# Masked products of a chunk: two heads on the array's row halves, a bank for each head

## The chip, the core and the metric

The kernel runs on one core of one Trainium2 chip. A core has a matrix engine (TensorE, PE in the profile, with its weight loads shown apart as PEld), a vector engine (VectorE, DVE), an activation engine (ScalarE, ACT), a general engine (GpSimd, POOL) and a queue that issues most of the DMAs (SyncE, SP). TensorE writes to PSUM, a small memory of 128 partitions in banks of 512 float32 columns; VectorE and ScalarE read it from there. The metric is device microseconds of one execution, as a median of several.

## What is computed

One inference step of a two-layer hybrid decoder: a convolution layer, then a layer of RWKV-7 time mixing, each followed by a squared-ReLU MLP. The prompt has 1024 tokens and 16 meta tokens in front, and 8 decoded sequences add one token each. The change lies in the time mixing of the prompt, the recurrence over tokens with 16 heads of size 64:

```python
def _wkv7_step(S, inp):
    r_t, w_t, k_t, v_t, kk_t, a_t = inp
    sa = jnp.einsum('bhvk,bhk->bhv', S, -kk_t)
    S = (S * w_t[:, :, None, :] + sa[..., None] * (kk_t * a_t)[:, :, None, :]
         + v_t[..., None] * k_t[:, :, None, :])
    y = jnp.einsum('bhvk,bhk->bhv', S, r_t)
    return S, y
```

The kernel doesn't step through the tokens. It takes them in 17 chunks (the 16 meta tokens, then 16 chunks of 64), and within a chunk it works with 64 x 64 matrices of products between tokens, masked to be triangular.

## The kernel before

**Layout.** The model's 1024 features are 8 blocks of 128 partitions (KT = 8). A block holds two heads: head q = 0 on partitions 0 to 63, head q = 1 on 64 to 127 (HALF[0] and HALF[1]). What a mixer stage computes for a chunk is written to the DRAM tensors d_ab (four 64-column vectors for each block), d_v and d_n, and read back by the recurrence.

**Stages.** The work before about 1100 us is the convolution layer and its MLP. Then the mixer runs over four token groups (`mixer_in`, whose projections are L865), and between its matmuls a `tick` advances the recurrence by a few steps. After the mixer the first group of the output projection and the second MLP runs (matmuls at L187 to L189), and its filler advances what is left of the recurrence, the decode step and the normalisation of the outputs. From about 2090 us on only the MLP is left. In these stages the order of TensorE's instructions is the order of the program (a manual schedule for that engine); the other engines' instructions are ordered by the scheduler that builds the kernel.

**One chunk.** `front(c)` loads a chunk and forms its products; `chunk(c)` goes on from there. Each is a generator that yields the credit its last step is worth, and `step(c + 1)` in the chunk before runs pieces of the next chunk's front early. In order:

- `front`: two tiles are loaded, `bk` (L1176 to L1179; stationary, its second head with its column halves swapped) and `xa` (one of two tiles taken in turn, with dimensions partition, block, head, 128 columns). Head q's data goes to `xa[HALF[q], :, q, :]` by SP's DMA (L1175). The other partition half of the same columns has to be zero, because a matmul over 128 partitions would otherwise add the other head's terms: the right 64 columns are zeroed once (L1139), the left 64 for each chunk by two POOL memsets (L1174), since the products below overwrite them.
- The products A (L1192): for each pair of blocks one bank, two matmuls of 128 x 128 weights with 256 moving columns (two heads of 128 columns). Then for each head ACT copies a 32 x 32 corner for both blocks to `no` (L1198) and VectorE writes the masked left half to the other head's partitions in `xa` (L1199); then VectorE writes the masked right halves of both heads to `nr` (L1200). After two of the four pairs the front yields.
- `chunk`: `gg` multiplies `no` with the transposed inverses (L1230; 32 x 32 tiles), `bT` transposes `bk` (L1253), `W` multiplies `xa`'s left half with the state and values `sv` (L1260), `po` (L1230) and `U` (L1276; 64 x 64 tiles) apply the inverse, `S` (L1285) makes the state's increment, and `Y` (L1292 with `xa`'s right half, L1295 with `nr`) the outputs.

**Banks.** A, gg, bT, W, po, U, S and Y, and the transposes of the output's normalisation, share one pool of three PSUM banks (tag "w"). A bank is taken again when all readers of its last tile are done. The mixer's own matmuls have four banks of their own.

**Other users of the queues.** On the mixer's side POOL issues the writes of d_ab, d_n and d_bv (L991, L1030, L1037); in the MLP it forms the low parts of the split weights (L162). `inverses` (L1153, L1154) works on VectorE over d_n and writes d_p.

Of the kernel before, what the change touches and what calls it, by code (L numbers as in the profile page):

```python
# [16 lines left out]
P = 128  # L17
D = 1024
KT = D // P
# [8 lines left out]
HS = 64  # L28
# [17 lines left out]
HALF = [slice(0, HS), slice(HS, P)]  # L46


def hybrid_step(tc, x_prompt, x_sample, state_conv, state_shift, state_wkv, meta_tokens,
# [8 lines left out]
    nc = tc.nc  # L58
    ctx = ExitStack()
    with ctx:  # L60
# [130 lines left out]
        def bank(name, tag="mm"):  # L191
            return cur[tag].tile([P, 512], F32, name=name, tag=tag)
# [191 lines left out]
        with ExitStack() as l0:  # L384
# [261 lines left out]
            with ExitStack() as s:  # L646
# [35 lines left out]
                for i, parts in enumerate((((1, rwkv_w1[0]), (4, rwkv_a1[0])), ((5, rwkv_g1[0]),))):  # L682
                    own, prev = (xin.tile([P, D], F32, name=f"lr{i}{s_}", tag="xt").rearrange("p (k c) -> p k c", k=KT) for s_ in "op")
                    w = P // len(parts)
# [22 lines left out]
        m_ar = masks.tile([P, 2 * HS], F32, name="m_ar")  # L707
# [459 lines left out]
        Q = [slice(32 * i, 32 * i + 32) for i in range(4)]  # L1167
        chunks = {}

        def front(c):  # L1170

            xa = xas[c % 2]
            for q in range(2):
                nc.gpsimd.memset(xa[HALF[1 - q], :, q, :HS], 0.0)  # L1174
                nc.sync.dma_start(xa[HALF[q], :, q, :], d_ab[c, HALF[q], :, 0, :])  # L1175
            bk = w_([P, KT, P], "bk", c)  # L1176
            nc.sync.dma_start(bk[HALF[0]], d_ab[c, HALF[0], :, 1, :])
            for i in range(2):
                nc.sync.dma_start(bk[HALF[1], :, i * HS:(i + 1) * HS], d_ab[c, HALF[1], :, 1, (1 - i) * HS:(2 - i) * HS])  # L1179
            nr, no = w_([P, KT, 2, HS], "nr", c, bufs=2), w_([P, KT, 32], "no", c)  # L1180
            p32 = w_([P, KT, 32], "p32", c, bufs=2)
            nc.sync.dma_start(p32, d_p[c].rearrange("k r t -> r k t"))

            vt = w_([P, KT, HS], "vt", c)
            for q in range(2):
                nc.sync.dma_start(vt[HALF[1 - q]], d_v[c * HS:(c + 1) * HS, :].rearrange("t (k q v) -> q t k v", q=2, v=HS)[q])
            yield RW[0]
            mk = m_ar.unsqueeze(1).broadcast_to([P, 2, P])
            for j in range(0, KT, 2):
                ps = bank(f"A{c}{j}", "w")  # L1190
                for i in range(2):
                    nc.tensor.matmul(ps[:, i * 2 * P:(i + 1) * 2 * P], bk[:, j + i, :],  # L1192
                                     xa[:, j + i].rearrange("p q x -> p (q x)"), start=True, stop=True)
                pv = ps.rearrange("p (i q x) -> p i q x", i=2, q=2)
                for q in range(2):

                    r_k = HALF[1 - q]
                    nc.scalar.copy(no[Q[2 * q], j:j + 2, :], pv[Q[2 * q], :, q, 32:64])  # L1198
                    nc.vector.tensor_mul(xa[r_k, j:j + 2, q, :HS], pv[r_k, :, q, :HS], mk[r_k, :, :HS])  # L1199
                nc.vector.tensor_mul(nr[:, j:j + 2].rearrange("p i q x -> p (i q) x"),  # L1200
                                     ps.rearrange("p (i x) -> p i x", x=P)[:, :, HS:],
                                     m_ar[:, HS:].unsqueeze(1).broadcast_to([P, 4, HS]))
                if j == 2:
                    yield RW[1]
            x32 = w_([P, KT, 32], "x32", c)
            nc.vector.transpose(flat(x32), flat(p32))
            chunks[c] = xa, bk, nr, no, p32, x32, vt
            yield RW[2]

        def step(c):  # L1210

            if c < NCH and c <= st["inv"]:
                if c not in fronts:
                    fronts[c] = front(c)
                next(fronts[c], None)
        fronts = {}

        def chunk(c):

            while c > st["inv"]:  # L1220
                yield None
            yield from fronts.setdefault(c, front(c))
            xa, bk, nr, no, p32, x32, vt = chunks.pop(c)
            sv, uv = st["sv"], st["uv"]
# [420 lines left out]
```

## Time and profile before

| what | us |
|---|---|
| median of 3 runs | 2832.22 |
| lowest and highest | 2829.05, 2835.45 |
| the profiled execution | 2823.53 |
| its span, first to last instruction | 2821.8 |

The mean granted TensorE clock was 0.977 of full speed. The profile's views are read as follows. Each group of instructions has its line in the kernel, its engine, its output and inputs, and its shape. A busy time is the sum over instructions; a wait is the time that an engine stood idle before an instruction, put down to what was done last of all that it waited for. A matmul's record reaches from its start to a modelled end, and neighbouring records overlap, so for the time that a matmul takes of TensorE the distance between starts is used. A float32 matmul leaves two records of matmul and two of weight load.

### The profile page before, as it was taken

The numbers are of one execution on the slowest core, as the hardware profiler recorded it, in microseconds if no ns is written. First come the engines' busy times: TensorE is split into PE (matmuls) and PEld (weight loads), VectorE is DVE, ScalarE is ACT, GpSimd is POOL, SyncE is SP. The second block draws the span as 40 slices with busy tenths as digits, with TensorE's granted clock in tenths as the row PEclk, the third lists the DMA queues.
The fourth block names the chain that finished last, engine by engine and source line by source line (L and its number), as shares of the span: only waits on it lengthen the run. The fifth ranks groups of instructions, "written<-read, shape, count | busy, mean of one in ns | idle before, by whom it ended". The sixth has DMA issues, their size and how long they took to land.

```text
span 2821.8 us, 51604 instructions
## 1 busy us (share of the span) xinstructions
PE 2669.5 (95%) x19594; PEld 2521.3 (89%) x19594; DVE 1785.4 (63%) x3586; ACT 1189.5 (42%) x2235; POOL 1520.2 (54%) x2100
## 2 busy tenths in 40 slices
PE   8999999999999899998999999978899999999998
PEld 8999999999999898786877778777899999999998
DVE  5999999996455545234756455588985564444444
ACT  5545444544354343233454454454444452222223
POOL 6686877887788775022212112375568773333332
PEclk9999999999999999999999999989899999999999
DMA  6663544454445642677767766766665542222211
GB/s 179 179 184 87 156 137 134 137 175 137 140 132 162 191 130 82 198 215 201 185 176 211 186 172 178 203 184 167 170 202 155 170 125 87 68 69 73 70 53 42
DMA packets 615862, 416.42 MB, mean 148 GB/s; under 512 B 104936, under 2 KB 558760, under 8 KB 615614
## 3 DMA queue, kind: packets, MB, share of 16 engines
q1 hardware_dynamic: 565996, 367.36, 46.0%
q10 hardware_dynamic: 41090, 19.93, 2.7%
q0 software_dynamic: 8528, 25.83, 2.6%
q8 instruction: 155, 2.54, 0.4%
q14 instruction: 93, 0.76, 0.1%
HBM read 345.60 MB, written 68.37 MB: 147 GB/s over the span
## 4 chain that ended last, share of the span: by engine, by line
PE 71%; DVE 13%; DMA 6%; issue 4%; ACT 3%; POOL 2%; SPq 0%; ACTq 0%; DVEq 0%; POOLq 0%
PE ps_in L187 8%; PE ps_in L189 8%; PE ps_in L188 8%; PE out L187 8%; PE out L189 8%; PE out L188 8%; PE pk L865 3%; PE pr L865 2%; PE pv L865 2%; POOL wo_lo L162 1%; DVE ni L1154 1%; DVE cv L519 1%; PE ps_o L189 1%; DVE tt L1153 1%; PE ps_o L188 1%
## 5 line engine op out<-in xcount | busy, mean ns | idle before, releaser
L162 POOL TENSOR_TENSOR wo_lo<-wo_raw,wo_hi 128x256 fp32r<-128x256 f32 x736 | 566.5, 802 | 267.5 <-ACT wo_hi L157 253.2
L162 POOL TENSOR_TENSOR wi_lo<-wi_raw,wi_hi 128x256 fp32r<-128x256 f32 x640 | 488.9, 796 | 285.8 <-ACT wi_hi L157 265.4
L187 PE MATMUL out<-hh,wo_hi 128*128 128x352 f32 (+2 forms) x1536 | 503.4, 328 | 19.8 <-DVE h L355 9.3
L355 DVE TENSOR_TENSOR h<-h,out 128x352 f32<-128x352 f32 (+2 forms) x768 | 387.7, 511 | 195.9 <-PE out L189 195.2
L189 PE MATMUL out<-hl,wo_hi 128*128 128x352 f32 (+2 forms) x1536 | 494.0, 324 | 7.2 <-DVE hl L141 7.2
L187 PE MATMUL ps_in<-m_h,wi_hi 128*128 128x352 f32 (+2 forms) x1536 | 496.2, 323 | 1.2 <-DVE h L355 1.2
L188 PE MATMUL out<-hh,wo_lo 128*128 128x352 f32 (+2 forms) x1536 | 495.3, 323 | 0.0
L189 PE MATMUL ps_in<-m_l,wi_hi 128*128 128x352 f32 (+2 forms) x1536 | 494.5, 322 | 0.1
L188 PE MATMUL ps_in<-m_h,wi_lo 128*128 128x352 f32 (+2 forms) x1536 | 492.6, 321 | 0.0
L519 DVE SCALAR_TENSOR_TENSOR cv<-u,wdw,cv 128x352 f32<-128x352 f32 (+2 forms) x720 | 377.2, 574 | 0.7
L157 ACT CAST wi_hi<-wi_raw 128x1024 fp32r<-128x1024 f32 x160 | 167.9, 1050 | 388.6 <-PE out L189 198.3
L157 ACT CAST wo_hi<-wo_raw 128x1024 fp32r<-128x1024 f32 x184 | 192.6, 1049 | 318.4 <-PE out L189 153.6
L187 PEld LDWEIGHTS out<-hh,wo_hi 128*128 128x128 f32 x1536 | 293.0, 191 | 26.0 <-DVE h L355 11.6
L189 PEld LDWEIGHTS out<-hl,wo_hi 128*128 128x128 f32 x1536 | 291.2, 190 | 8.9 <-DVE hl L141 8.8
L188 PEld LDWEIGHTS out<-hh,wo_lo 128*128 128x128 f32 x1536 | 292.4, 190 | 0.7
L187 PEld LDWEIGHTS ps_in<-m_h,wi_hi 128*128 128x128 f32 x1536 | 290.1, 189 | 3.2 <-issue 1.7
L188 PEld LDWEIGHTS ps_in<-m_h,wi_lo 128*128 128x128 f32 x1536 | 289.4, 188 | 1.0
L189 PEld LDWEIGHTS ps_in<-m_l,wi_hi 128*128 128x128 f32 x1536 | 288.7, 188 | 1.2 <-DVE m_l L285 0.4
L342 DVE SCALAR_TENSOR_TENSOR r<-ps_in,rs_m 128x352 f32<-128x352 f32 (+2 forms) x192 | 98.4, 516 | 238.7 <-PE ps_in L189 235.0
L141 DVE TENSOR_TENSOR hl<-s,hh 128x352 fp32r<-128x352 f32 (+2 forms) x192 | 147.1, 767 | 106.2 <-ACT hh L140 106.0
L344 ACT ACTIVATE s<-r 128x352 f32<-128x352 f32 (+2 forms) x192 | 93.8, 491 | 129.1 <-DVE r L342 128.5
L865 PE MATMUL pv<-mx,wv_raw 128*128 128x256 f32 (+2 forms) x512 | 125.3, 393 | 2.7 <-ACT rk L1049 2.7
(356 smaller groups left out, 4874.4 us busy)
## 6 DMA issues: line engine op xcount, KB each, us to landing
wi_raw<-in_w_mlp_in_dram SPq DMA_DIRECT2D x160, 512.0 KB
wo_raw<-in_w_mlp_out_dram SPq DMA_DIRECT2D x160, 512.0 KB
wk_raw<-in_rwkv_w_k_dram SPq DMA_DIRECT2D x32, 512.0 KB
wr_raw<-in_rwkv_w_r_dram SPq DMA_DIRECT2D x32, 512.0 KB
wv_raw<-in_rwkv_w_v_dram SPq DMA_DIRECT2D x32, 512.0 KB
d_ab<-ab POOLq DMA_DIRECT2D x32, 512.0 KB, 5.0
pg_raw<-in_conv_w_pw_dram SPq DMA_DIRECT2D x24, 512.0 KB
pa_raw<-in_conv_w_pw_dram SPq DMA_DIRECT2D x24, 512.0 KB
```

Of the source, the lines that this page charges most:

```text
L141: eng_lo.tensor_sub(lo, src, hi.bitcast(F32))
L157: nc.scalar.copy(hi[:, :a * b], raw[:, :a * b])
L162: eng_lo.tensor_sub(lo[:, cs], raw[:, cs], hi[:, cs].bitcast(F32))
L187: nc.tensor.matmul(ps, w[0], act[0], start=first, stop=False)
L188: nc.tensor.matmul(ps, w[1], act[0], start=False, stop=False)
L189: nc.tensor.matmul(ps, w[0], act[1], start=False, stop=last)
L342: nc.vector.scalar_tensor_tensor(r[:, :n], ps[:, :n], 0.0, rs()[:, :n], op0=ALU.max, op1=ALU.mult)
L344: nc.scalar.activation(s[:, :n], r[:, :n], AF.Square)
L355: nc.vector.tensor_add(hv[:, 4 * i + m, :], hv[:, 4 * i + m, :], ps[:, :n])
L519: nc.vector.scalar_tensor_tensor(acc[m][:, :n], ug[:, m, j:j + n], wdw[:, m, j:j + 1], acc[m][:, :n], op0=ALU.mult, op1=ALU.add)
L865: nc.tensor.matmul(ps[:, :n], w[:, k, :], act[k], start=k == 0, stop=k == KT - 1)
L1153: nc.vector.tensor_mul(o, ni[:, :j, j:j + 1].broadcast_to([B, j, wd]), ni[:, j:j + 1, j + 1:top].broadcast_to([B, j, wd]))
```

## The change

In `front`, the memsets of `xa`'s left columns go. The products are formed for four blocks at a time instead of two: two banks, one for each head, and for each block and head one matmul of 64 x 128 weights (the head's partitions of `bk`) with 128 moving columns (the head's partitions of `xa`), at row 0 or row 64 of the array, the heads in turn. The ACT copies and the VectorE products each cover four blocks of one head; the two copies come first, then two products into `xa`, then two into `nr`. The front yields after the first four blocks, as before. Per chunk this makes 16 matmuls instead of 8, four copies instead of 8, and 8 VectorE products instead of 12, with the same number of elements in all. The zeros in `xa`'s right columns, which `Y` needs, stay.

```diff
             for q in range(2):
-                nc.gpsimd.memset(xa[HALF[1 - q], :, q, :HS], 0.0)
                 nc.sync.dma_start(xa[HALF[q], :, q, :], d_ab[c, HALF[q], :, 0, :])
...
-            mk = m_ar.unsqueeze(1).broadcast_to([P, 2, P])
-            for j in range(0, KT, 2):
-                ps = bank(f"A{c}{j}", "w")
-                for i in range(2):
-                    nc.tensor.matmul(ps[:, i * 2 * P:(i + 1) * 2 * P], bk[:, j + i, :],
-                                     xa[:, j + i].rearrange("p q x -> p (q x)"), start=True, stop=True)
-                pv = ps.rearrange("p (i q x) -> p i q x", i=2, q=2)
+            mask = lambda x: m_ar[:, x].unsqueeze(1).broadcast_to([P, 4, HS])
+            for j in range(0, KT, 4):
+                ps = [bank(f"A{c}{j}{q}", "w") for q in range(2)]
+                for i in range(4):
+                    for q in range(2):
+                        nc.tensor.matmul(ps[q][:, i * P:(i + 1) * P], bk[HALF[q], j + i, :], xa[HALF[q], j + i, q, :],
+                                         start=True, stop=True, tile_position=(64 * q, 0))
+                pv = [t.rearrange("p (i x) -> p i x", x=P) for t in ps]
+                js = slice(j, j + 4)
                 for q in range(2):
-
+                    nc.scalar.copy(no[Q[2 * q], js, :], pv[q][Q[2 * q], :, 32:64])
+                for q in range(2):
                     r_k = HALF[1 - q]
-                    nc.scalar.copy(no[Q[2 * q], j:j + 2, :], pv[Q[2 * q], :, q, 32:64])
-                    nc.vector.tensor_mul(xa[r_k, j:j + 2, q, :HS], pv[r_k, :, q, :HS], mk[r_k, :, :HS])
-                nc.vector.tensor_mul(nr[:, j:j + 2].rearrange("p i q x -> p (i q) x"),
-                                     ps.rearrange("p (i x) -> p i x", x=P)[:, :, HS:],
-                                     m_ar[:, HS:].unsqueeze(1).broadcast_to([P, 4, HS]))
-                if j == 2:
+                    nc.vector.tensor_mul(xa[r_k, js, q, :HS], pv[q][r_k, :, :HS], mask(slice(0, HS))[r_k])
+                for q in range(2):
+                    nc.vector.tensor_mul(nr[:, js, q, :], pv[q][:, :, HS:], mask(slice(HS, P)))
+                if j == 0:
                     yield RW[1]
```

## The prediction

> **What bounds the kernel now.** The page first: the span, the busy shares, and the chain that ended last by engine.
>
> ```profile
> span 2821.8 us, 51604 instructions
> PE 2669.5 (95%) x19594; PEld 2521.3 (89%) x19594; DVE 1785.4 (63%) x3586; ACT 1189.5 (42%) x2235; POOL 1520.2 (54%) x2100
> PE 71%; DVE 13%; DMA 6%; issue 4%; ACT 3%; POOL 2%; SPq 0%; ACTq 0%; DVEq 0%; POOLq 0%
> ```
>
> TensorE is the bound of the whole, but an average says nothing about the stages in which the changed lines run. The next two views are the busy time by stage (columns: stretch, its length, then busy us and count for PE, PEld, DVE, ACT, POOL, then granted clock, DMA share, GB/s), for everything and then for the products' line alone (PE and PEld only).
>
> ```profile
> 1340.00:1820.00 480.00, 452.00 (x4854) 379.55 (x4852) 284.84 (x690) 225.44 (x589) 104.52 (x190) 0.98 0.70 186
> 1820.00:2090.00 270.00, 227.25 (x2456) 210.94 (x2455) 233.34 (x477) 129.58 (x263) 156.09 (x188) 0.90 0.65 171
> ...
> 1340.00:1820.00 480.00, 46.11 (x192) 35.91 (x192) 0.98 0.70 186
> 1820.00:2090.00 270.00, 19.30 (x80) 14.52 (x80) 0.90 0.65 171
> ```
>
> Stage one, the mixer, holds 192 of the 272 records, or 12 of the 17 chunks (16 records each); there TensorE works 452 of 480 us and VectorE 285. Stage two, the first group of the output projection and MLP, holds the last 5 chunks; TensorE works 227 of 270 us and VectorE 233. So in stage one a shorter matmul is nearly a shorter stage, in stage two it may be hidden by VectorE. What TensorE waits for there because of these products, four lines for each stage (us in total, times, longest):
>
> ```profile
> PE gg L1230 <- ACT no L1198: 3.0, 6, 0.7
> PE A L1192 <- DVE nr L1200: 2.4, 1, 2.4
> PE bT L1253 <- DVE nr L1200: 0.8, 2, 0.5
> PE Y L1292 <- DVE nr L1200: 0.6, 1, 0.6
> ...
> PE gg L1230 <- ACT no L1198: 9.5, 6, 4.4
> PE Y L1292 <- DVE nr L1200: 9.0, 3, 3.9
> PE bT L1253 <- DVE nr L1200: 2.5, 4, 1.2
> PE gg L1230 <- DVE nr L1200: 2.4, 1, 2.4
> ```
>
> These are the waits for the evacuation of the products: 6.8 us in stage one, 23.4 us in stage two.
>
> **The matmuls.** Each float32 matmul leaves two records, so the 136 matmuls of L1192 are the x272 below. The rows after it, from the order of time on TensorE (start, length, group), show one half of a chunk's products (A, x8) in its surroundings, and a block whose operands already lie on two row halves (U).
>
> ```profile
> L1192 PE MATMUL A<-xa,bk x272: 378/379/483, 1342.1 to 2047.4; 128*128 128x256 f32 x136
> ...
> 1405.68 1.46 PE L865 MATMUL pk<-mx,wk_raw 128*128 128x256 f32 x6
> 1407.07 1.15 PE L1276 MATMUL U<-w,p 64*64 64x64 f32 x32
> 1408.15 1.56 PE L865 MATMUL pk<-mx,wk_raw 128*128 128x256 f32 x6
> 1409.55 1.89 PE L1192 MATMUL A<-xa,bk 128*128 128x256 f32 x8
> 1411.28 1.03 PE L865 MATMUL pk<-mx,wk_raw 128*128 128x256 f32 x4
> 1412.14 0.59 PE L880 MATMUL pn<-sq,hsel 128*128 128x256 f32 x2
> ```
>
> Lengths overlap, so I use starts. A half of A takes 1411.28 - 1409.55 = 1.73 us, 0.216 for each of 8 records; the next four records take 0.86, again 0.215. After the change a half is 8 matmuls of 64 rows by 128 columns with 128 moving columns: 16 records, each 0.108 us long if it had the array alone (half the columns). No row shows that form, so I bound it.
>
> Below: both halves at once and no loss at the edges, 16 x 0.108 / 2 = 0.86 us, a gain of 0.87 per half. Above: one after the other, for which the transposes are the nearest row, 128 columns of weights and 128 moving columns on the one array:
>
> ```profile
> 1393.18 1.09 PE L1253 MATMUL bT<-ident,bk 128*128 128x128 f32 x8
> 1394.11 3.62 PE L865 MATMUL pr<-mx,wr_raw 128*128 128x256 f32 x16
> ```
>
> 0.93 us for 8 records, 0.116 each; 16 of them 1.86 us. To this come the edges. U shows these: six L865 records should take 6 x 0.215 = 1.29, but from 1405.68 to U are 1.39, and after U, from 1408.15 to 1409.55, 1.40. So entering and leaving the split array cost about 0.10 + 0.11 us of their neighbours' time. The upper end is 1.86 + 0.21 = 2.07, a loss of 0.34 per half.
>
> I take U itself: float32, two row halves in the same alternating order, and the same streamed columns (32 x 64 = 16 x 128). It takes 1.08 us plus the edges, 1.29. The gain is 1.73 - 1.29 = 0.44 us per half; 24 halves in stage one give 10.6 us, 10 in stage two 4.4. U's tiles share no array columns while the new ones do and are told apart by bank only; that is the unproven step.
>
> On the edges: the Trainium skill, TensorEngine Tiling (Array Packing), Key Properties, states that a change of tiling mode drains the engine, which speaks against putting a new mode into a stream of full-array matmuls. U's neighbours agree, at the 0.2 us already counted; without that rule the sum would be some 7 us better (34 x 0.21).
>
> **The weight loads.** They double from 8 to 16 records a half, each still 128 columns wide. The rows: U's loads, two row halves with 64 columns each.
>
> ```profile
> 1364.11 1.01 PEld L1276 LDWEIGHTS U<-w,p 64*64 64x64 f32 x32 [0.33 <-DVE ni L1154]
> ```
>
> 1.01 / 32 = 0.032 us a load, inside the block's time; twice the columns at half the count leaves the total. I add nothing; if the cover goes, they are the 0.116 us a record of the upper end.
>
> **The evacuation.** Per half, before: 4 ACT copies (L1198), 4 small VectorE products (L1199), 2 large (L1200). After: 2 copies of 32x128, and 4 products of 256 elements, on 64 and on 128 partitions.
>
> ```profile
> L1198 ACT COPY no<-A x136: 185/203/205, 1343.1 to 2052.9; 32x64 f32<-32x64 f32 x136
> L1199 DVE TENSOR_TENSOR xa<-A,m_ar x136: 230/285/296, 1343.9 to 2054.1; 64x128 f32<-64x128 f32 x136
> L1200 DVE TENSOR_TENSOR nr<-A,m_ar x68: 403/406/410, 1345.2 to 2054.3; 128x256 f32<-128x256 f32 x68
> L1238 ACT COPY gg<-gg x34: 363/364/367, 1352.5 to 2054.6; 32x256 f32<-32x256 f32 x34
> L1174 POOL MEMSET xa<- x34: 518/520/547, 1128.1 to 1988.8; 64x512 f32 x34
> ```
>
> VectorE: 4 x 0.285 + 2 x 0.406 = 1.95 us becomes 4 x 0.406 = 1.62, 0.33 less a half. ACT: 0.81 becomes 2 x 0.257 (between 0.203 at 64 elements and 0.364 at 256), 0.30 less. More matters the order. On one bank copies and products take turns:
>
> ```profile
> DVE xa L1199 <- ACT no L1198: 34.7, 47, 2.6
> ...
> ACT no L1198 <- DVE xa L1199: 27.0, 33, 3.3
> ...
> ACT no L1198 <- DVE xa L1199: 30.9, 16, 6.6
> ```
>
> The first two are stage one's, the third stage two's. The second head's copy waits for the first head's product; with a bank for each head it only waits for the matmuls, and gg (which needs all copies) no longer has VectorE in its path. So gg's waits on `no`, 3.0 and 9.5 us, can go; those for a bank held by `nr` (the other lines) only shorten, since the last product still ends some 4 x 0.41 = 1.6 us after the copies. I return 4 of 6.8 us in stage one and 8 of 23.4 in stage two, between nothing and all.
>
> **Memsets and DMA.** The 34 memsets are 34 x 0.520 = 17.7 us of POOL, which is 104.5 of 480 us busy in stage one; there I count nothing. The same POOL queue stood behind them 43.8 us:
>
> ```profile
> POOL xa L1174 <- PE W L1260: 43.8, 5, 14.8
> ```
>
> behind it lie the writes of d_ab, d_n and d_bv, which are wanted a chunk later; were that cover gone, the gain is bounded by those 43.8, and I take 0. The same count of DMAs is issued from SP, in the same order. Nothing new is stored.
>
> **The sum.** Stage one: 10.6 + 4 = 14.6, of which I let a quarter go, since the chain of waits in that stage also runs through other work:
>
> ```profile
> by line: issue 9.0%; PE pr L865 8.4%; PE pv L865 6.7%; DVE ni L1154 5.1%; PE pk L865 5.0%; DVE tt L1153 4.6%; PE A L1192 3.1%; DMA d_p<-ni 2.9%; DMA p<-d_p 2.0%; PE bT L1253 1.9%; PE W L1260 1.8%; PE S L1285 1.8%; DMA ni<-d_n 1.6%; PE U L12
> ```
>
> (ni, tt and their DMAs, the inversions, are 16% there.) That leaves 11. Stage two: half of 4.4, since VectorE is as busy as TensorE, and the 8: 10. Together 21 us. The profiled execution took 2823.5 us (span 2821.8 and 1.7 around it), so it would become 2802.5; the median of the runs shown is 2832.2, 8.7 more, and I apply the difference to that: 2811.
>
> **The rivals.**
> - *The whole of it comes through* (chance 0.10): no absorption, all 30 us of evacuation waits gone: 15 + 30 = 45, 2787. For it: TensorE's 95%. Against it: `nr` still holds its banks.
> - *VectorE and the inversions pace both stages* (0.16): only the cut in VectorE's work in stage two (10 x 0.33 = 3.3) and a quarter of stage one's matmuls (2.6) show: 6 less, 2826. For it: 233 against 227 us. Against it: 452 of 480.
> - *The row halves don't overlap* (0.14), so the edit's purpose isn't met: 34 x 0.34 = 11.6 slower, less stage one's 4, about 8: 2840. It decides where a record costs over (1.73 - 0.21) / 16 = 0.095 us. For it: no row has two tiles over the same columns. Against it: U's pace. The Trainium skill, TensorE: Matmul & The Clock Gate, LDWEIGHTS, says a load's time follows its columns and not its rows, 107 ns at 128 by its formula; by it alone 16 loads make 1.7 us and this rival is the outcome. U's 0.032 us against its 53 ns for 64 columns shows loads of different row halves overlapping, which the same page's part on packing small matmuls allows.
> - *Both banks at once* (0.08), slower: a half now needs two of the pool's three banks at its first two matmuls, where before it took the second after four records, 0.86 us later. In the second half that bank is the one S leaves through VectorE. If each half stood 0.86 us for it, 34 x 0.86 = 29 against 15 gained: 14 slower, 2846. It decides once a half waits over 0.44 us more. Against it: A waited for a bank once in stage one, 2.4 us.
>
> **How the numbers follow.** The forecast has 0.52, with its own range 2797 to 2823 (the absorbed quarter and half none or doubled). Leaving out half of the first rival and most of the last two leaves 0.2 outside 2788 to 2836. About 0.2% (5.7 us) is what a measurement of this kernel can tell from no change. Faster by more: 0.52 + 0.10 + 0.06 of the second rival = 0.68; within: its other 0.10 and a little of the third, 0.12; slower: 0.20.
>
> **What would show it.** Right: 544 records at L1192, a half's start-to-next 1.0 to 1.2 us, gg no longer waiting for `no`, ACT not waiting for `xa`, TensorE's busy time lower by some 15 us. Wrong: a half over 1.7 us (no overlap); waits of A on `fs`, `w1` or `nr` of more than 10 us (banks); or a half of 1.1 us with the stages as long as before (VectorE).

## The result and the profile after

| | before, us | after, us |
|---|---|---|
| median (4 runs each) | 2831.94 | 2815.85 |
| lowest to highest | 2829.05 to 2835.45 | 2812.34 to 2817.97 |
| the profiled execution | 2823.53 | 2817.97 |
| its span | 2821.8 | 2816.3 |

The ratio is 0.9944 with a 95% interval of 0.9931 to 0.9958: 16 us faster, where 21 were forecast. The two profiles differ by 5.6 us only, because that of before was of an uncommonly short execution, below all four runs of the table. So stages are compared further down with a second profile of the kernel before. Now the views that answer to those of the prediction, all of the kernel after. The page:

```profile
span 2816.3 us, 51957 instructions
PE 2661.4 (95%) x19866; PEld 2510.5 (89%) x19866; DVE 1776.7 (63%) x3518; ACT 1180.9 (42%) x2167; POOL 1499.7 (53%) x2066
```

The busy time by stage, for everything and then for the products alone:

```profile
1340.00:1820.00 480.00, 447.96 (x5038) 371.51 (x5040) 282.74 (x652) 220.75 (x544) 90.28 (x168) 0.96 0.70 186
1820.00:2090.00 270.00, 225.84 (x2569) 208.56 (x2570) 236.18 (x462) 129.43 (x247) 155.73 (x184) 0.91 0.67 178
...
1340.00:1820.00 480.00, 28.74 (x384) 23.98 (x384) 0.96 0.70 186
1820.00:2090.00 270.00, 13.06 (x160) 10.57 (x160) 0.91 0.67 178
```

The products' own busy time fell from 65.4 to 41.8 us, but TensorE's over the span by 8.1 only (2669.5 to 2661.4). This is the short execution again: its mean clock was 0.977, against 0.972 here. A second profile of the kernel before, at 0.972, has TensorE busy for 2680.0 us, and one of the kernel after 2660.8. The order of time on TensorE, with U as the measure beside A:

```profile
1412.05 1.15 PE L1276 MATMUL U<-w,p 64*64 64x64 f32 x32
1413.13 1.56 PE L865 MATMUL pk<-mx,wk_raw 128*128 128x256 f32 x6
1414.62 1.16 PE L1192 MATMUL A<-xa,bk 64*128 64x128 f32 x16
1415.71 1.13 PE L865 MATMUL pk<-mx,wk_raw 128*128 128x256 f32 x4
1416.68 0.59 PE L880 MATMUL pn<-sq,hsel 128*128 128x256 f32 x2
```

A half takes 1415.71 - 1414.62 = 1.09 us, U 1.08, and the four records behind A take 0.97 instead of 0.86. Between U and A the six records take 1.49, where before, with a full-array A, they took 1.40. The row halves overlap, and entering and leaving the split array costs 0.09 and 0.11 us, all close to the forecast from U. Some of what TensorE and its weight loads (PEld) then wait for, from 1330 to 2090 us, the two longest and those that bear on the products:

```profile
PE bT L1253 <- DVE nr L1202: 12.6, 7, 3.6
PE pb L756 <- ACT vv L1067: 11.1, 5, 4.5
PE Y L1292 <- DVE nr L1202: 4.4, 3, 2.8
PE A L1192 <- DVE nr L1202: 3.2, 1, 3.2
PE A L1192 <- DVE fs L1303: 2.4, 2, 1.6
...
PEld gg L1230 <- ACT no L1197: 2.2, 8, 0.3
```

The matmuls of gg no longer stand idle for `no` (12.5 us before); bT's wait for a bank has grown from 3.3 to 12.6. The evacuation, its sizes and what ACT waits for:

```profile
L1197 ACT COPY no<-A x68: 237/256/257, 1348.5 to 2046.5; 32x128 f32<-32x128 f32 x68
L1202 DVE TENSOR_TENSOR nr<-A,m_ar x68: 402/415/426, 1349.5 to 2049.8; 128x256 f32<-128x256 f32 x68
...
ACT no L1197 <- PE A L1192: 33.1, 17, 5.5
```

There is no line left in which a copy waits for `xa`; before, these were 57.9 us.

### The profile page after: what moved, and what is told of

It is laid out like the page before. It is cut to its first block, busy times and chain, and to the rows that moved or that the text cites. A ratio compares the mean times of both kernels' runs of the same rounds, so it can differ in the third digit from the quotient of the medians.

```text
span 2816.3 us, 51957 instructions
## 1 busy us (share of the span) xinstructions
PE 2661.4 (95%) x19866; PEld 2510.5 (89%) x19866; DVE 1776.7 (63%) x3518; ACT 1180.9 (42%) x2167; POOL 1499.7 (53%) x2066
## 4 chain that ended last, share of the span: by engine, by line
PE 72%; DVE 13%; DMA 6%; issue 3%; ACT 3%; POOL 2%; SPq 0%; ACTq 0%; DVEq 0%; POOLq 0%
PE out L187 8%; PE ps_in L189 8%; PE ps_in L187 8%; PE out L189 8%; PE ps_in L188 8%; PE out L188 8%; PE pk L865 3%; PE pr L865 3%; PE pv L865 2%; DVE cv L519 1%; POOL wo_lo L162 1%; PE ps_o L189 1%; DVE tt L1153 1%; PE ps_o L188 1%; PE ps_o L187 1%
## 5 line engine op out<-in xcount | busy, mean ns | idle before, releaser
L1030 POOL DMA_DIRECT2D d_n<-n x32 | 24.4, 764 | 212.9 <-DVE n L1020 141.0
```

## Experiments

Each run was timed against the kernel before in five rounds, both on one chip; medians in us, ratios with their 95% interval.

| run | median | before | ratio |
|---|---|---|---|
| before_again | 2833.23 | 2831.43 | 1.0008 (0.9997 to 1.0019) |
| after_again | 2818.23 | 2831.43 | 0.9952 (0.9934 to 0.9971) |
| after_serial | 2818.22 | 2831.43 | 0.9962 (0.9947 to 0.9977) |
| after_order | 2814.30 | 2831.43 | 0.9949 (0.9933 to 0.9964) |
| before_evac | 2818.22 | 2831.90 | 0.9949 (0.9934 to 0.9965) |
| before_copies | 2821.46 | 2831.90 | 0.9963 (0.9951 to 0.9975) |
| after_memset | 2814.64 | 2831.90 | 0.9941 (0.9928 to 0.9953) |
| after_double | 2844.84 | 2831.90 | 1.0045 (1.0033 to 1.0058) |
| after_vv | 2825.21 | 2833.97 | 0.9965 (0.9951 to 0.9978) |
| evac_vv | 2825.70 | 2833.97 | 0.9969 (0.9957 to 0.9981) |
| serial_order | 2820.58 | 2833.97 | 0.9952 (0.9937 to 0.9967) |
| after_turns | 2817.32 | 2834.42 | 0.9942 (0.9923 to 0.9960) |

The theory at the outset: the shorter matmuls and the shorter evacuation each bring about half. The rival: one of the two brings nearly all.

**before_again, after_again: the two kernels once more.**

> The kernel before, for a second profile beside the first, whose execution (2823.5 us) was 8 us shorter than the median. If time is nothing but a fixed schedule, stage lengths repeat within 1 us: 713 us from the mixer's first projection to the first matmul of the output projection, 240 us from there to the transposes of the final state. If the clock's half-rate windows after idle gaps of TensorE set the spread, as I hold, the mixer is some 4 to 8 us longer here and holds more such windows than the 4 (17 us) of the first profile after its first products.

> The changed kernel once more, beside the others on one chip. Expected ratio to the kernel before 0.992 to 0.996. Mixer some 10 us shorter than in the kernel before of the same call; if the gain is only in stage two, as the first two profiles read (1.8 us in the mixer, 6.4 us behind it), the mixers agree within 3 us.

Busy time by stage in these profiles and three that follow. The first row of each pair reaches from the first product to the first matmul of the output projection (the rest of the mixer), the second from there to the transposes of the final state (stage two). In order: before_again, after_again, after_serial, before_copies, and the first row alone for before_evac.

```profile
1343.10:1847.80 504.70, 466.88 (x4951) 390.69 (x4949) 293.02 (x708) 236.15 (x615) 107.17 (x201) 0.96 0.70 186
1847.80:2088.90 241.10, 208.97 (x2266) 195.11 (x2266) 218.86 (x445) 114.76 (x230) 144.73 (x170) 0.90 0.64 166
```
```profile
1342.40:1842.30 499.90, 457.12 (x5143) 377.82 (x5142) 286.67 (x660) 229.61 (x567) 95.84 (x179) 0.96 0.71 188
1842.30:2077.50 235.20, 202.32 (x2344) 187.85 (x2345) 215.50 (x418) 113.14 (x211) 140.88 (x162) 0.93 0.64 170
```
```profile
1341.80:1845.10 503.30, 464.31 (x5144) 388.29 (x5143) 286.60 (x660) 232.53 (x569) 95.17 (x179) 0.96 0.71 186
1845.10:2076.40 231.30, 204.18 (x2346) 189.36 (x2346) 213.66 (x417) 112.32 (x211) 142.91 (x162) 0.95 0.65 172
```
```profile
1341.80:1847.40 505.60, 462.63 (x4951) 388.42 (x4950) 294.96 (x708) 239.28 (x617) 107.18 (x201) 0.96 0.70 185
1847.40:2079.00 231.60, 205.56 (x2264) 189.70 (x2265) 217.80 (x434) 115.87 (x231) 145.19 (x170) 0.94 0.64 171
```
```profile
1345.80:1849.10 503.30, 464.63 (x5143) 396.83 (x5141) 285.18 (x655) 229.94 (x567) 106.92 (x200) 0.96 0.71 186
```

The kernel before took 504.7 us in the mixer row, against 498.4 between the same instructions in its first profile, where the granted clock was 0.98 and not 0.96. With the part of the mixer ahead of the first product the difference is smaller, 716.3 and 713.2 us, so less than the 4 to 8 expected; stage two repeats (241.1 and 240.5). Ahead of 1825 us the mixer row of the second profile holds eight stretches of 3.4 us at about half clock, the first holds four; four such stretches more cost 4 x 3.4 / 2 = 6.8 us, which is about the 6.3 of the row. From these two profiles the change is worth 4.8 us in the mixer row, where both have a clock of 0.96, and 5.9 in stage two, where the clock was 0.90 before and 0.93 after. The first is between the two expectations. One profile of each says this to within a few us, no better.

**after_serial: the same instructions, the row halves one after the other.**

```diff
-                for i in range(4):
-                    for q in range(2):
+                for q in range(2):
+                    for i in range(4):
```

> The changed kernel with only the order of the products changed: head 0's four blocks, then head 1's, so that records of one row half follow one another and the halves cannot overlap but at the boundary. If overlap of the row halves makes the gain: a half of a chunk's products takes 1.7 to 1.9 us from start to next start instead of 1.09, 34 halves give 21 to 28 us of TensorE, and the time rises by 12 to 28 us over the changed kernel, to about the kernel before or above it. If the evacuation and the absent memsets make the gain: within 5 us of the changed kernel.

Its order of time on TensorE:

```profile
1411.25 1.71 PE L1192 MATMUL A<-xa,bk 64*128 64x128 f32 x16
1412.89 1.13 PE L865 MATMUL pk<-mx,wk_raw 128*128 128x256 f32 x4
```

A half now takes 1.64 us, a little less than expected and 0.55 more than in alternating order, or 34 x 0.55 = 18.7 us of TensorE. The time is that of after_again. So the matmul term of the prediction, 15 of 27 us before absorption, doesn't show in the time of this pair. By stage it does: the mixer row is 3.4 us longer than after_again's and stage two 3.9 us shorter.

**before_evac: no row halves, the new evacuation.** Full-array weights and zero halves with their memsets, one matmul for each block and head into the head's bank:

```diff
-  nc.tensor.matmul(ps[q][:, i * P:(i + 1) * P], bk[HALF[q], j + i, :], xa[HALF[q], j + i, q, :],
-                   start=True, stop=True, tile_position=(64 * q, 0))
+  nc.tensor.matmul(ps[q][:, i * P:(i + 1) * P], bk[:, j + i, :], xa[:, j + i, q, :],
+                   start=True, stop=True)
```

> Full-array matmuls with zero halves and memsets as before, one matmul for each block and head, but the banks by head and the evacuation of the changed kernel: no row halves at all. A half should take about 16 x 0.108 to 0.116 = 1.73 to 1.86 us on TensorE, as long as before or longer. If the evacuation makes the gain (the serial order kept it): 2816 to 2823 us. If the row halves make it: 2830 us or more.

```profile
1345.79 1.95 PE L1193 MATMUL A<-xa,bk 128*128 128x128 f32 x16
1347.57 1.03 PE L865 MATMUL pv<-mx,wv_raw 128*128 128x256 f32 x4
```

A half takes 1.78 us, as long as before (1.73), and the kernel is 13.7 us faster than before all the same.

**before_copies: the kernel before, with both copies of a bank ahead of its products.**

```diff
                 for q in range(2):
-                    r_k = HALF[1 - q]
                     nc.scalar.copy(no[Q[2 * q], j:j + 2, :], pv[Q[2 * q], :, q, 32:64])
+                for q in range(2):
+                    r_k = HALF[1 - q]
                     nc.vector.tensor_mul(xa[r_k, j:j + 2, q, :HS], pv[r_k, :, q, :HS], mk[r_k, :, :HS])
```

> The kernel before with one reordering: both copies of a bank, then its products, so that ACT and VectorE no longer take turns on it; sizes, banks, matmuls and memsets as before. If the turns alone cost the time: 2817 to 2825 us, and the waits of the copies for xa (58 us) go. If it takes the larger pieces, the bank for each head or the absent memsets: 2828 to 2833 us.

What is left of ACT's wait at the copies, and of the waits of TensorE for the products in stage two:

```profile
ACT no L1196 <- PE A L1192: 34.5, 33, 3.2
ACT no L1196 <- issue: 3.7, 6, 2.2
...
PE bT L1253 <- DVE nr L1200: 8.4, 5, 3.4
PE Y L1292 <- DVE nr L1200: 2.2, 2, 1.5
```

10.4 us for moving two statements. The rows above place it: stage two went from 241.1 to 231.6, while the mixer stayed (504.7 and 505.6). What was lost there can be seen in the first profile of the kernel before, in the order of time near the end of stage two:

```profile
2049.94 0.30 DVE L1199 TENSOR_TENSOR xa<-A,m_ar 64x128 f32<-64x128 f32 x1
...
2050.68 0.43 ACT L1198 COPY no<-A 32x64 f32<-32x64 f32 x2
...
2051.54 1.03 DVE L141 TENSOR_TENSOR hl<-s,hh 128x328 fp32r<-128x328 f32 x1
...
2052.60 0.29 DVE L1199 TENSOR_TENSOR xa<-A,m_ar 64x128 f32<-64x128 f32 x1
...
2052.93 0.20 ACT L1198 COPY no<-A 32x64 f32<-32x64 f32 x1 [1.31 <-DVE xa L1199]
...
2053.18 0.31 PE L1230 MATMUL gg<-x,no 32*32 32x32 f32 x6 [0.38 <-ACT no L1198]
```

The last copy (0.20 us) waits for a product of VectorE, which stands behind 1 us of the MLP's work on VectorE; ACT idles 1.31 us ahead of it, and whatever follows on ACT waits too; then gg starts.

**after_turns: the old order in the program, on a bank for each head.**

```diff
                     nc.scalar.copy(no[Q[2 * q], js, :], pv[q][Q[2 * q], :, 32:64])
-                for q in range(2):
                     r_k = HALF[1 - q]
```

> The changed kernel with the old order in the program: copy and product of head 0, then copy and product of head 1, on a bank for each head. If the cost of the old order was that both engines share one bank, so that the second copy has to wait for the first product, there is nothing to wait for here: the copies' wait for xa stays at 0 and the time within 0.2% of 2816. If the order in the program itself sets it, ACT waits for VectorE again (20 us or more) and the time rises by 6 to 12 us.

2817.3 us, ratio 0.9942, and the copies wait for A (32.3 us) and never for `xa`. With a bank for each head the order of the statements doesn't matter; with one bank it did. So it was the shared bank that made the copy wait for the product.

**after_memset: the memsets put back (one line, L1174, which runs for each of the two heads).**

> The changed kernel with the two POOL memsets of each chunk put back, which nothing needs. If they and the POOL queue behind them cost time: 3 to 10 us over the changed kernel (2815 to 2818). If they were hidden, as the prediction has it: within 0.2% of it.

2814.6 us, within the changed kernel's runs. They were hidden.

**after_order, serial_order: head 0's bank freed earlier.** VectorE's products head by head, in the changed kernel and in after_serial:

```diff
-                for q in range(2):
                     nc.vector.tensor_mul(nr[:, js, q, :], pv[q][:, :, HS:], mask(slice(HS, P)))
```

> The changed kernel with VectorE's four products taken head by head (xa, nr of head 0, then of head 1), so that head 0's bank is free one product, 0.41 us, earlier. If the banks held by nr still cost time, the waits of bT and Y for nr (17 us in the changed kernel) fall by 3 to 8 us and the time by 1 to 5 us. If not, the time stays within 0.2%.

> The changed kernel with head 0's matmuls first, then head 1's, and VectorE's products head by head, so that head 0's bank is emptied while head 1's matmuls run. If the banks held by nr cost more than the 0.55 us of matmul time a half: 2808 to 2814 us. If the two orders are worth as little as each alone: 2814 to 2820.

2814.3 and 2820.6 us, ratios 0.9949 and 0.9952: neither differs from the changed kernel, though serial_order ended just above both of its expected ranges. In after_order bT waited 12.8 us for `nr` and Y 7.6, 20 together, where a fall from 17 was one of the outcomes. The bank's release one product earlier is worth nothing that shows.

**after_double: each product matmul issued twice.**

```diff
-                for i in range(4):
+                for i in range(8):
+                    i %= 4
```

> The changed kernel with each product matmul issued twice: 32 records a half, about 0.9 us more, 34 x 0.9 = 31 us of TensorE in all, and nothing else changed. If TensorE's time counts fully: 2847 us. If only a quarter of it or less counts, as between the serial and the overlapped order: 2817 to 2826 us.

```profile
1342.12 2.06 PE L1193 MATMUL A<-xa,bk 64*128 64x128 f32 x32
1344.11 1.13 PE L865 MATMUL pv<-mx,wv_raw 128*128 128x256 f32 x4
```
```profile
PE bT L1254 <- DVE nr L1203: 15.6, 10, 4.7
PE Y L1293 <- DVE nr L1203: 12.0, 3, 5.8
PE A L1193 <- DVE nr L1203: 6.8, 3, 3.3
```

1.99 us a half, 0.9 more, and 26.6 us more time (against after_again; 30.2 against after_memset, on the same chip), nearly the whole 31. But beside the matmul time the waits for banks grew, and every product comes 0.9 us later: Y's from 4.4 to 12.0 us. So this run doesn't show that TensorE's time alone counts fully in this direction; it shows that longer products, with what comes later behind them, do harm.

**after_vv, evac_vv: v's copy out of PSUM on VectorE.** In both kernels:

```diff
-                nc.scalar.copy(vv[:, :n], ps[:, :n])
+                nc.vector.tensor_copy(vv[:, :n], ps[:, :n])
```

> The changed kernel with the 32 copies of v's projection out of PSUM (L1067) on VectorE instead of ACT. In the mixer of the changed kernel TensorE waits 11 to 12 us for this copy, and 8 in the kernel before. If ACT's late copy is what takes back the mixer's saving in matmul time, the wait falls below 5 us and the mixer after its first products goes from 499 us to 490 or less, the time to 2805 to 2811. If another wait follows at once, the mixer stays within 3 us and the time within 0.2% of 2816.

> The same move in the kernel with full-array products and the new evacuation (503 us in the mixer after its first products, 4 more than the changed kernel). If ACT's copy hid the row halves' saving, the distance to after_vv grows from 4 to 8 to 12 us in the mixer. If not, it stays at 4 or less.

A theory that fell: both became slower, 2825.2 and 2825.7 us. The mixer's waits of after_vv and its row by stage:

```profile
PE pb L756 <- DVE vv L1067: 7.3, 2, 5.5
PE pb L756 <- ACT vt L1003: 5.4, 2, 3.9
```
```profile
1342.00:1850.90 508.90, 460.03 (x5144) 380.82 (x5143) 294.82 (x683) 223.78 (x544) 96.57 (x179) 0.95 0.70 184
```

The same matmul now waits for VectorE and for the next copy, 12.7 us together, and the row is 9 us longer than after_again's; which wait made it longer isn't shown. In evac_vv it took 510.3 us, so the distance fell to 1.4 us, where 8 to 12 would have spoken for the theory. It isn't ACT's lateness alone that takes the matmul time back.

## Why the prediction came out right, and where it did not

- *The half of a chunk's products.* Forecast 1.08 us and 0.21 of edges, from U. Measured 1.09, and 0.09 ahead of it and 0.11 behind. Right, and the tiles that share array columns overlap as U's do.
- *What that is worth.* Forecast 15.0 us of TensorE and 10 of it in the time after absorption: 8 in the mixer (three quarters of 10.6) and 2 in stage two (half of 4.4). This is the term that was mis-sized. The three kernels with a bank for each head and no overlap gained 13.2, 13.7 and 13.4 us (after_serial, before_evac, serial_order), the five with overlap 16.1, 13.2, 17.1, 17.3 and 17.1 (after, after_again, after_order, after_memset, after_turns). On the mean, 13.4 and 16.2: some 3 us. The eight ratios taken together give 2.5 us with a 95% interval of -0.7 to 5.7, so even the 3 are not settled by the times. TensorE's time differs by far more: 18.7 us against after_serial, and against before_evac 34 x (1.78 - 1.09 - 0.20 of edges) = 17. The profiles show where it went, one for each kernel, in the rows used above (lengths in us):

| kernels | mixer row | stage two |
|---|---|---|
| before_again | 504.7 | 241.1 |
| before_copies | 505.6 | 231.6 |
| no overlap: after_serial, before_evac, serial_order | 503.3, 503.3, 507.9 | 231.3, 232.6, 230.2 |
| overlap: after, after_again, after_order, after_memset, after_turns | 498.0, 499.9, 496.9, 498.8, 498.5 | 234.1, 235.2, 234.9, 233.6, 234.7 |

In the mixer all five with overlap are shorter, by 6 us on the mean, which is not far from the 8 forecast; TensorE is busy 10 us less there (454 to 457 against 464 to 467). In stage two all five are longer, by 3 us, where 2 shorter was forecast. So the step that failed is stage two's: the forecast let half of the saved matmul time through there, and the stage grew. What goes with it: bT waits 12.1 to 13.6 us for `nr` in that stage instead of 7.1 to 9.8, and the granted clock is 0.91 to 0.93 instead of 0.93 to 0.95. That these two are the cause is not shown. With v's copy on VectorE (after_vv against evac_vv) the same pair of rows is 1.4 us shorter and 4.1 longer, so the mixer's 6 us depend on what else waits there.

- *The evacuation.* Forecast 12 us, 4 in the mixer and 8 in stage two, between nothing and 30, and 11 of it after absorption. Measured 13.7 with the full array (before_evac), 10.4 of it by the order on one bank alone (before_copies). The step was right in stage two, where before_copies' profile has 9.5 us. The mixer's 4 don't show: its row took 504.7 us before, 505.6 in before_copies and 503.3 to 507.9 in the three without overlap. In the time the evacuation brings more of the whole than forecast: four fifths (13.4 of 16.2), not half.
- *The banks.* gg's wait went, and the waits for banks held by `nr` were forecast to shorten only. bT's grew, from 3.3 to 12.6 us: gg starts earlier and bT now arrives ahead of the last product. Most of that came with the evacuation (8.4 us in stage two of before_copies), the rest with the shorter matmul. Both banks at once, a rival, decided nothing: A waited 2.4 us for `fs`, in two waits, and 3.2 for `nr`, in one, against 2.4 for `nr` before.
- *Memsets, weight loads, DMAs.* Forecast nothing; after_memset shows it for the first, the length of A's half for the second. No run varies the DMAs.
- *The rivals.* The whole of it comes through: no, 2787 was not reached, and `nr` still held its banks. No overlap: excluded by A's 1.09 us, and after_serial shows that it would not have been slower either; its price of 8 us more than before took 1.86 us a half and the edges, where 1.64 were measured, and left out the evacuation's gain in stage two. VectorE and the inversions setting the pace: its 2.6 us for the matmuls are near the some 3 of the times, but not as the sum of 6 gained in the mixer and 3 lost in stage two, and it left out the evacuation.

So the time, 16 us less where 21 were forecast, fell well inside a wide range (9 to 35 us less), in part by luck: too much for the matmuls (10 for some 3) and a little too little for the evacuation (11 for 13.4) cancelled in part.

## What to carry to other kernels

Before a matmul is made shorter, look at what its results are evacuated by: here two statements on one PSUM bank, in which two engines waited for each other in turn, cost 10 us, and the shorter matmuls themselves (1.73 to 1.09 us a half), on the engine with 95% of busy time, brought some 3. A bank for each reader's chain, or the reads of the engine with the free queue first, takes such turns away; both did so here (after_turns, before_copies). And one experiment that undoes each half of a change alone separates what a sum of terms cannot.

## What was not expected of the hardware

An idle gap can cost TensorE more than its length. Of the kernel after, a matmul that waited, and the stages around it (the last three columns are clock, DMA share, GB/s):

```profile
1483.25 0.58 PE L756 MATMUL pb<-r16h,hspread 128*128 128x256 f32 x1 [3.52 <-ACT vv L1067]
```
```profile
1478.60:1483.20 4.60, 1.13 (x36) 0.64 (x34) 3.94 (x9) 4.50 (x12) 0.00 (x0) 1.00 0.40 94
1483.20:1486.60 3.40, 3.35 (x10) 2.35 (x12) 3.37 (x9) 0.27 (x1) 1.29 (x2) 0.51 1.07 312
1486.60:1490.00 3.40, 3.40 (x105) 3.33 (x106) 2.51 (x5) 1.26 (x3) 0.35 (x2) 0.99 0.18 54
```

After 3.5 us of idling the granted clock is 0.51 for 3.4 us. The Trainium skill, TensorE: Matmul & The Clock Gate, Part 1, states half rate after an idle window of about 3.4 us, and this gap agrees. A shorter one did it too, in the same profile:

```profile
1347.75 0.70 PE L1034 MATMUL pk<-rk,hsum 128*128 128x256 f32 x2
1349.67 0.39 PE L756 MATMUL pb<-r16h,hspread 128*128 128x256 f32 x1 [1.22 <-ACT vv L1067]
```
```profile
1350.00:1353.40 3.40, 3.40 (x14) 2.40 (x14) 3.40 (x12) 0.00 (x0) 1.30 (x2) 0.52 0.80 282
```

1.22 us of idling were followed by 3.4 us at 0.52. The length alone doesn't decide: in the first profile of the kernel before, 3.04 us of idling were followed by full clock.

```profile
1698.62 0.71 PE L880 MATMUL pn<-sq,hsel 128*128 128x264 f32 x2 [3.04 <-ACT sq L888]
```
```profile
1698.60:1702.00 3.40, 3.38 (x17) 3.01 (x18) 2.10 (x2) 1.69 (x2) 0.00 (x0) 1.00 1.21 242
```

So matmul time that turns into waits can be paid for again in clock, and the mixer's clock, 0.98 in one execution of the kernel before and 0.96 in another, went with 6 us of that stage. That the clock is what kept the shorter matmuls from paying is argued, not shown: in the mixer the overlapped and the serial kernel had 0.96 alike, and in stage two, where they had 0.93 and 0.95, the clock may follow the waits as well as make them.
